# Decoder layer on one core: new prices in the planner that interleaves its side work (table loads, row sums, powers on POOL, the turn back to main matmuls)

## The chip, the cores and the metric

The kernel runs on one core of a Trainium2 chip. The metric is device time in microseconds (us) of one execution. TensorE (PE) multiplies matrices, VectorE (DVE), ScalarE (ACT) and GpSimd (POOL) do the elementwise work, SyncE (SP) issues the transfers.

## What is computed

One decoder layer on 256 rows of width 1024, float32, in three blocks:

```python
h = rms_norm(x, norm_mix_pre)
qa, ka, va, qd, kd, vd, zd, bd, ad, ga, gd = split(h @ w_in)
ya = moba_attention(rope(qa), rope(ka), va)              # 8 heads of 128, causal
yd = gated_deltanet(qd, kd, vd, zd, bd, ad)              # 8 heads of 128, chunks of 64
merged = sigmoid(ga) * (ya @ w_o_attn) + sigmoid(gd) * (yd @ w_o_delta)
x = x + rms_norm(merged @ w_out, norm_mix_post)
h = rms_norm(x, norm_ffn_pre)
out = x + rms_norm((silu(h @ w_gate) * (h @ w_up)) @ w_down, norm_ffn_post)
```

In the gated delta branch q, k and v go through a causal convolution, a silu and, for q and k, a norm over each head; a decay matrix `exp` of cumulative sums gates a chunked recurrence with state S; its output `o` is normalised per head and multiplied by `silu(z)`.

## The kernel before

**Main work.** The large products keep PE busy. Each weight piece of 128x1024 (some of 824 columns) is loaded into one of 4 raw buffers (`wr`), and `split_to` (L427) splits it into a high and a low part, `wh` on ACT and `wl` on DVE, in one of 5 buffers each. A split is asked for three pieces ahead of use. A product takes three matmuls, high x high, high x low and low x high, each of them 256, 412 or 512 columns wide. The main generators (`unit_c`, `unit_z`, `unit_a`, `unit_g`, `unit_oa`, `unit_od`) run over the column blocks of `w_in` and then the output products, and hand control back after every three matmuls.

**Side work.** Between them side generators put small steps: `decays` (L636, decay matrices `d_dc` and their transposes `d_dT`), `dn_tile` (L676, per head group of four and half t of the rows: squares of q and k summed by ACT into `tiny`, the power -1/2 on POOL, the normalised keys `d_kn` on DVE, their transposes, evicted by ACT as `d_kh`, the product of `d_kh` with itself, and a blockwise inverse in `h_a`, `h_T`, `h_U`), `dn_out` (L784, the recurrence: `d_vb`, `h_r`, `d_vn`, state `d_S`, output `d_oA`, whose squares, power and scaling come before its transposes), and `attn` (L892). `q_aq` and `q_ak` are the attention's queries and keys; `q_gt` the sigmoid gates; `scr` takes the squares that nobody reads.

**Order.** A planner, `Flow` (L138), sets the order while the program is written. It keeps a clock for PE (`t`) and one each for ACT, DVE, POOL and the DMA (`clk`). `account` (L165) adds a price to an engine's clock for every operation and notes when its output is ready; `pe` (L196) adds a price to `t` for every matmul. A side generator that has yielded `At(tiles)` gets a due time, the ready time of these tiles plus 50 ns (`MARGIN`, L215). After every three main matmuls `pump` (L228) resumes each side generator whose due time `t` has passed. `issue` (L270) keeps side matmuls behind the last main matmul. The planner's clocks do not wait for buffers of the weights; the framework then lays out each engine's queue, and every engine runs its queue in order. The prices before:

```python
        if kind == "A":
            c = (51 if psum else 94) + 0.833 * n
            c += 93 * sum(isinstance(kw.get(k), bass.AP) for k in ("scale", "bias", "accum_out"))
...
        else:
            c = 90 + (180 * n if ALU.pow in args else 1.15 * n if op == "affine_select" else 1.9 * n)
```

All operations of ACT, DVE, POOL and SP pass through `Engine.__call__` and appear in the profile as L132; matmuls are L290 and transposes L294.

Of the kernel before, what the change touches and what calls it, by code (L numbers as in the profile page):

```python
# [13 lines left out]
AF = mybir.ActivationFunctionType  # L14
ALU = mybir.AluOpType
# [11 lines left out]
NFR = DFF // 512  # L27
PSUM = bass.MemoryType.PSUM
MARGIN = 50
STAG = 0  # L30
WARM = 5
DEC = 6
# [49 lines left out]
class Slots:  # L82
    def __init__(self, pool, name, n, fl):
        self.pool, self.name, self.fl = pool, name, fl
        self.idle = list(range(n))
        self.rel = [0.0] * n
        self.owner = {}
        self.low = n
# [28 lines left out]
def free_size(ap):  # L117
    n = 1
    for d in ap.shape[1:]:
        n *= d  # L120
    return n
# [16 lines left out]
class Flow:  # L138
    def __init__(self):
        self.t = 0.0  # L140
        self.side = []
        self.n = 0
        self.done = set()
        self.log = []
        self.in_side = self.fresh = False
        self.last = None
        self.rdy, self.used = {}, {}
        self.clk = {"A": 0.0, "V": 0.0, "P": 0.0, "D": 1700.0}

# [15 lines left out]
    def account(self, kind, op, args, kw):  # L165
        aps = [a for a in list(args) + list(kw.values()) if isinstance(a, bass.AP)]
        out = kw.get("out", args[0])
        outs = [out]
        if kw.get("accum_out") is not None:
            outs.append(kw["accum_out"])  # L170
        ins = [a for a in aps if all(a is not o for o in outs)]
        n = free_size(out)
        if op == "dma_start":
            st = max(self.clk["D"], self.start(outs, []))
            self.clk["D"] = st + n * 128 * 4 / 341.0
            self.touch(outs, [], self.clk["D"] + 1000, 0)
            return
        psum = any(a.space == PSUM for a in ins)
        if kind == "A":
            c = (51 if psum else 94) + 0.833 * n  # L180
            c += 93 * sum(isinstance(kw.get(k), bass.AP) for k in ("scale", "bias", "accum_out"))
        elif kind == "V":
            if op in ("tensor_copy", "memset", "tensor_scalar"):
                c = 65 + (1.042 if psum else 0.55) * n
            elif op == "scalar_tensor_tensor":
                c = 130 + 1.042 * n
            else:
                n = max([n] + [free_size(a) for a in ins])
                c = 69 + 1.042 * n
        else:  # L190
            c = 90 + (180 * n if ALU.pow in args else 1.15 * n if op == "affine_select" else 1.9 * n)
        st = max(self.clk[kind], self.start(outs, ins))
        self.clk[kind] = st + c
        self.touch(outs, ins, st + c, 60)

    def pe(self, out, l, r, cost):  # L196
        self.t = max(self.t, self.start([out], [l, r])) + cost
        self.touch([out], [l, r], self.t, 200)

# [4 lines left out]
    def step(self, s):  # L204
# [10 lines left out]
        if isinstance(w, At):  # L215
            del s[4:]
            s[0] = max(self.rdy.get(n, 0.0) for n in w.names) + MARGIN
        elif callable(w):
# [34 lines left out]
def build(nc, tc, ctx, A):  # L253
# [756 lines left out]
    def unit_c(u):  # L1010
# [13 lines left out]
        if dns[g] == 6:  # L1024
            fl.add(("dn", g, 0), dn_tile(g, 0))
            fl.add(("dn", g, 1), later(STAG, dn_tile(g, 1)))
            fl.add(("dno", g), after(("dn", g, 0), dn_out, g))
# [327 lines left out]
    def later(ns, gen):  # L1355
        yield ns
        yield from gen

    def after(name, f, *args):
        while name not in fl.done:  # L1360
            yield 500
        yield from f(*args)
# [27 lines left out]
```

## Time and profile before

| | |
|---|---|
| time, median of 3 runs (lowest, highest) | 549.74 us (549.35, 549.91) |
| the profiled execution: time, span | 549.29 us, 547.6 us |
| PE busy, share of the span | 534.8 us, 98% |
| DVE, ACT, POOL busy | 368.1, 315.0, 26.4 us |
| mean granted clock of TensorE, share of full speed | 0.994 |
| ACT table loads | 12, 1283 ns each |
| power on POOL, 128x4 / 128x1, mean | 1012 / 665 ns |

The span runs from the first to the last instruction; the execution's own time is 1.7 us longer. PE is nearly always busy, so an interval in which PE waits is the time that an order can save or lose; the busy time of other engines counts only where PE waits for them.

### The profile page before, as it was taken

The page shows a single profiled execution, that of the slowest core. Times are in us where ns is not written, and L with a number is a line of the kernel's source. Part 1 is how long each engine was busy: PE and PEld are TensorE (multiplying, and loading weights), DVE is VectorE, ACT ScalarE, POOL GpSimd, SP SyncE. Part 2 cuts the span into 40 slices and gives each one's busy share as a digit, 9 for nine tenths or more (in the row PEclk, how much of TensorE's full clock was granted, in tenths as well). Part 3 has the DMA queues.
Part 4 walks back from the last instruction along what each step waited for, and adds up shares of the span by engine and source line. Part 5 has one row for each costly group of instructions (what it writes and reads, how often), then busy time and mean ns, then how long its engine had stood idle before and what let it go on. Part 6 is the DMA issues. An engine that isn't in the chain of part 4 may idle for free.

```text
span 547.6 us, 8378 instructions
## 1 busy us (share of the span) xinstructions
PE 534.8 (98%) x3156; PEld 460.6 (84%) x3156; DVE 368.1 (67%) x650; ACT 315.0 (58%) x553; POOL 26.4 (5%) x38
## 2 busy tenths in 40 slices
PE   7999999899999999999999999999999999999995
PEld 5988898898989888899889988778888888888884
DVE  4899876895879787866577567586465554554434
ACT  6868658487654965786526544585444544443331
POOL 0000002200000230000000000010000000000000
PEclk8999999999999999999999999999999999999998
DMA  8947765245455252244465766257666665555612
GB/s 258 255 149 216 218 197 150 78 117 167 129 168 158 78 167 64 63 148 155 131 201 187 247 210 195 77 158 259 202 189 193 180 197 176 181 189 192 193 38 78
DMA packets 63035, 90.40 MB, mean 165 GB/s; under 512 B 3233, under 2 KB 35090, under 8 KB 62994
## 3 DMA queue, kind: packets, MB, share of 16 engines
q1 hardware_dynamic: 62994, 89.86, 53.4%
q8 instruction: 25, 0.41, 0.3%
q14 instruction: 16, 0.13, 0.1%
HBM read 88.80 MB, written 1.05 MB: 164 GB/s over the span
## 4 chain that ended last, share of the span: by engine, by line
PE 85%; DVE 4%; ACT 3%; DMA 3%; issue 2%; POOL 2%; SPq 0%; POOLq 0%; DVEq 0%; ACTq 0%
PE b_m L290 73%; PE b_s L290 8%; PE b_s L294 2%; PE b_m L294 2%; DMA q_x<-in_x 1%; DVE wl L132 1%; POOL tiny L132 1%; DMA K<-in_shape_k 1%; DMA wr<-in_w_in 1%; ACT wh L132 1%; ACT L132 0%; DVE h_a L132 0%; DVE q_vT L132 0%; SPq L132 0%; ACT d_js L132 0%
## 5 line engine op out<-in xcount | busy, mean ns | idle before, releaser
L132 DVE TENSOR_TENSOR wl<-wr,wh 128x1024 fp32r<-128x1024 f32 (+3 forms) x168 | 197.8, 1184 | 120.8 <-ACT wh L132 116.9
L132 ACT ACTIVATE wh<-wr 128x1024 fp32r<-128x1024 f32 (+3 forms) x168 | 171.8, 1030 | 151.6 <-PE b_m L290 142.9
L290 PE MATMUL b_m<-wh,q_fh 128*128 128x512 f32 x264 | 103.5, 392 | 0.5 <-DVE q_fl L132 0.5
L290 PE MATMUL b_m<-wl,q_fh 128*128 128x512 f32 x264 | 103.0, 390 | 0.0
L290 PE MATMUL b_m<-wh,q_fl 128*128 128x512 f32 x264 | 102.7, 390 | 0.0
L290 PE MATMUL b_m<-wh,q_hh 128*128 128x512 f32 (+2 forms) x208 | 83.1, 400 | 1.0 <-ACT wh L132 1.0
L290 PE MATMUL b_m<-wl,q_hh 128*128 128x512 f32 (+2 forms) x208 | 78.8, 379 | 0.0
L290 PE MATMUL b_m<-wh,q_hl 128*128 128x512 f32 (+2 forms) x208 | 78.8, 379 | 0.0
L290 PEld LDWEIGHTS b_m<-wh,q_fh 128*128 128x128 f32 x264 | 49.6, 188 | 11.0 <-DVE q_fl L132 1.0
L290 PEld LDWEIGHTS b_m<-wl,q_fh 128*128 128x128 f32 x264 | 49.6, 188 | 10.7 <-DVE wl L132 0.7
L290 PEld LDWEIGHTS b_m<-wh,q_fl 128*128 128x128 f32 x264 | 49.5, 188 | 10.3
L290 PE MATMUL b_m<-q_hh,wh 128*128 128x256 f32 x192 | 56.3, 293 | 0.0
L290 PE MATMUL b_m<-q_hl,wh 128*128 128x256 f32 x192 | 54.4, 283 | 0.0
L290 PE MATMUL b_m<-q_hh,wl 128*128 128x256 f32 x192 | 54.4, 283 | 0.0
L290 PEld LDWEIGHTS b_m<-wh,q_hh 128*128 128x128 f32 x208 | 39.5, 190 | 5.4 <-ACT wh L132 1.5
L290 PEld LDWEIGHTS b_m<-wh,q_hl 128*128 128x128 f32 x208 | 39.5, 190 | 5.3
L290 PEld LDWEIGHTS b_m<-wl,q_hh 128*128 128x128 f32 x208 | 39.6, 190 | 4.3 <-DVE wl L132 0.5
L132 POOL TENSOR_TENSOR tiny<-tiny,mhalf 128x4 f32<-128x4 f32 (+1 forms) x20 | 17.4, 873 | 471.3 <-DVE tiny L132 471.3
L290 PEld LDWEIGHTS b_m<-q_hh,wh 128*128 128x128 f32 x192 | 36.7, 191 | 0.4
L290 PEld LDWEIGHTS b_m<-q_hl,wh 128*128 128x128 f32 x192 | 36.7, 191 | 0.3
L290 PEld LDWEIGHTS b_m<-q_hh,wl 128*128 128x128 f32 x192 | 36.7, 191 | 0.1
L132 ACT ACTIVATE h_U<-b_s 128x256 f16<-128x256 f32 (+1 forms) x28 | 11.5, 415 | 10.9 <-PE b_s L290 10.9
(204 smaller groups left out, 718.0 us busy)
## 6 DMA issues: line engine op xcount, KB each, us to landing
wr<-in_w_in SPq DMA_DIRECT2D x56, 512.0 KB, 3.8
wr<-in_w_down SPq DMA_DIRECT2D x22, 512.0 KB, 3.3
wr<-in_w_gate SPq DMA_DIRECT2D x20, 512.0 KB, 3.7
wr<-in_w_up SPq DMA_DIRECT2D x20, 512.0 KB, 3.7
wr<-in_w_in SPq DMA_DIRECT2D x12, 412.0 KB, 3.4
wr<-in_w_o_attn SPq DMA_DIRECT2D x8, 512.0 KB, 4.4
wr<-in_w_o_delta SPq DMA_DIRECT2D x8, 512.0 KB, 4.2
wr<-in_w_out SPq DMA_DIRECT2D x8, 512.0 KB, 3.7
```

Source lines behind the costliest of these rows:

```text
L132: r = f(*args, **kw)
L290: issue(lambda: PE.matmul(out, l, r, start=start, stop=stop))
L294: issue(lambda: PE.transpose(out, in_, idn))
```

## The change

Four prices of the planner change; no instruction is added or taken away. ACT: a sum over a row (`accum_out`) is priced at 205 ns in place of 93, and a pointer as scale or bias at 93, of which the larger one counts; a function of another family than the one before it (`TABLES`: Exp and Sigmoid are one, Silu another) adds 1283 ns. POOL: a power costs 540 + 107 n in place of 90 + 180 n ns, n elements per row. PE: the first main matmul after side matmuls costs 85 ns more.

```diff
--- before.py
+++ after.py
@@ -27,6 +27,7 @@
 NFR = DFF // 512
 PSUM = bass.MemoryType.PSUM
 MARGIN = 50
+TABLES = {AF.Exp: "e", AF.Sigmoid: "e", AF.Silu: "s"}
 STAG = 0
 WARM = 5
 DEC = 6
@@ -142,8 +143,8 @@
         self.n = 0
         self.done = set()
         self.log = []
-        self.in_side = self.fresh = False
-        self.last = None
+        self.in_side = self.fresh = self.turned = False
+        self.last = self.fam = None
         self.rdy, self.used = {}, {}
         self.clk = {"A": 0.0, "V": 0.0, "P": 0.0, "D": 1700.0}
 
@@ -178,7 +179,12 @@
         psum = any(a.space == PSUM for a in ins)
         if kind == "A":
             c = (51 if psum else 94) + 0.833 * n
-            c += 93 * sum(isinstance(kw.get(k), bass.AP) for k in ("scale", "bias", "accum_out"))
+            c += max(93 * any(isinstance(kw.get(k), bass.AP) for k in ("scale", "bias")),
+                     205 * (kw.get("accum_out") is not None))
+            fam = TABLES.get(args[2])
+            if fam and fam != self.fam:
+                self.fam = fam
+                c += 1283
         elif kind == "V":
             if op in ("tensor_copy", "memset", "tensor_scalar"):
                 c = 65 + (1.042 if psum else 0.55) * n
@@ -188,12 +194,15 @@
                 n = max([n] + [free_size(a) for a in ins])
                 c = 69 + 1.042 * n
         else:
-            c = 90 + (180 * n if ALU.pow in args else 1.15 * n if op == "affine_select" else 1.9 * n)
+            c = 540 + 107 * n if ALU.pow in args else 90 + (1.15 * n if op == "affine_select" else 1.9 * n)
         st = max(self.clk[kind], self.start(outs, ins))
         self.clk[kind] = st + c
         self.touch(outs, ins, st + c, 60)
 
     def pe(self, out, l, r, cost):
+        if self.turned and not self.in_side:
+            cost += 85
+        self.turned = self.in_side
         self.t = max(self.t, self.start([out], [l, r])) + cost
         self.touch([out], [l, r], self.t, 200)
```

PE's queue is the same up to about 95 us of the profiled execution and from about 300 us on. Between them, three places.

**PE, the keys of the first head group, around 96 us.** `b4_m` is the main product, `b0_s` and the like are banks of side steps, `d0_kn` and `d1_kn` the normalised keys of the two halves. Before:

```order
L290 MATMUL b4_m_1147<-q4_hh1_126,wl28_1032 128x256
L290 MATMUL b4_m_1147<-q4_hh1_126,wh28_1031 128x256
L290 MATMUL b4_m_1147<-q5_hl1_127,wh28_1031 128x256
L290 MATMUL b4_m_1147<-q4_hh1_126,wl28_1032 128x256
L294 MATMUL b2_s_1180<-ident_71,d0_kn_1130 128x128 x4
L294 MATMUL b3_s_1187<-ident_71,d1_kn_1132 128x128 x4
L294 MATMUL b7_s_1194<-ident_71,q11_aq0_610 128x128 x4
L290 MATMUL b4_m_1147<-q4_hh1_126,wh28_1031 128x256
```

After:

```order
L299 MATMUL b4_m_1147<-q4_hh1_126,wl28_1032 128x256
L303 MATMUL b2_s_1180<-ident_71,q11_aq0_610 128x128 x4
L299 MATMUL b4_m_1147<-q4_hh1_126,wh28_1031 128x256
L299 MATMUL b4_m_1147<-q5_hl1_127,wh28_1031 128x256
L299 MATMUL b4_m_1147<-q4_hh1_126,wl28_1032 128x256
L299 MATMUL b4_m_1147<-q4_hh1_126,wh28_1031 128x256
L299 MATMUL b4_m_1147<-q5_hl1_127,wh28_1031 128x256
L299 MATMUL b4_m_1147<-q4_hh1_126,wl28_1032 128x256
L303 MATMUL b3_s_1192<-ident_71,d0_kn_1136 128x128 x4
L303 MATMUL b7_s_1199<-ident_71,d1_kn_1138 128x128 x4
L303 MATMUL b1_s_1206<-ident_71,q13_ak0_854 128x128 x4
```

The second four `q11_aq0` transposes and six main matmuls now stand ahead of the two groups of key transposes.

**ACT and DVE, the keys of the second head group, around 194 us.** `wh55` to `wh58` are weight pieces, `scr` the squares (bank `b7_s_2263` after, `b0_s_2263` before, for the second half's keys), `h5_r16` reads `d16_vb`. ACT before:

```order
L132 ACTIVATE scr_97,tiny_96<-b0_s_2263 128x128 x3
L132 ACTIVATE d8_dT10_2363<-b2_s_2358 128x512
L132 ACTIVATE h5_r16_2410<-d16_vb_1101 128x512
L132 ACTIVATE q17_ak1_2376<-b3_m_2169,tiny_96 128x512
L132 ACTIVATE wh56_2412<-wr56_2226 128x1024
L132 ACTIVATE wh57_2500<-wr57_2298 128x1024
L132 ACTIVATE d2_vn_2409<-b1_s_2421 128x512
L132 ACTIVATE h6_r16_3098<-d15_vb_2282 128x512
L132 ACTIVATE d4_dc11_2437<-b3_s_2434 128x512
L132 ACTIVATE d3_kh_2445<-b6_s_2440 128x512
L132 ACTIVATE d10_kh_2452<-b4_s_2447 128x512
L132 ACTIVATE wh58_2561<-wr58_2331 128x1024
```

ACT after:

```order
L133 ACTIVATE scr_97,tiny_96<-b7_s_2263 128x128
L133 ACTIVATE q17_ak1_2345<-b5_m_2169,tiny_96 128x512
L133 ACTIVATE scr_97,tiny_96<-b7_s_2263 128x128
L133 ACTIVATE wh56_2409<-wr56_2226 128x1024
L133 ACTIVATE scr_97,tiny_96<-b7_s_2263 128x128
L133 ACTIVATE h6_r16_3101<-d15_vb_2282 128x512
L133 ACTIVATE d14_dT10_2400<-b3_s_2395 128x512
L133 ACTIVATE h5_r16_2451<-d16_vb_1101 128x512
L133 ACTIVATE wh57_2441<-wr57_2298 128x1024
L133 ACTIVATE wh58_2532<-wr58_2331 128x1024
L133 ACTIVATE d2_kh_2432<-b5_s_2427 128x512
L133 ACTIVATE d4_kh_2439<-b3_s_2434 128x512
```

The evictions of the keys (`d2_kh`, `d4_kh`) come after `h5_r16` and two weight pieces, where they (`d3_kh`, `d10_kh`) came ahead of `wh58`. The last square comes after `wh56`.

DVE before:

```order
L132 TENSOR_SCALAR tiny_96<-tiny_96 128x4
L132 SCALAR_TENSOR_TENSOR d16_vb_1101<-b6_s_2342,tiny_96,d16_vb_1101 128x128 x3
L132 TENSOR_SCALAR tiny_96<-tiny_96 128x4
L132 SCALAR_TENSOR_TENSOR d16_vb_1101<-b6_s_2342,tiny_96,d16_vb_1101 128x128
L132 TENSOR_TENSOR d1_oA_2356<-b4_s_2351,tiny_96 128x512
L132 TENSOR_TENSOR d5_kn_2369<-b7_s_2252,tiny_96 128x512
L132 TENSOR_TENSOR d6_kn_2371<-b0_s_2263,tiny_96 128x512
```

DVE after:

```order
L133 SCALAR_TENSOR_TENSOR d16_vb_1101<-b4_s_2376,tiny_96,d16_vb_1101 128x128
L133 TENSOR_TENSOR q17_ak1_2345<-h6_m_2353 128x4x32
L133 TENSOR_SCALAR tiny_96<-tiny_96 128x4
L133 SCALAR_TENSOR_TENSOR d16_vb_1101<-b4_s_2376,tiny_96,d16_vb_1101 128x128
L133 TENSOR_TENSOR d8_kn_2371<-b7_s_2263,tiny_96 128x512
L133 SCALAR_TENSOR_TENSOR d16_vb_1101<-b4_s_2376,tiny_96,d16_vb_1101 128x128 x2
```

The last two of the four quarters of `d16_vb` come after the second `kn`, where all four came ahead of both.

**ACT and DVE, the last output of the second head group, around 295 us.** `d6_oA` before and `d8_oA` after are that output; the squares read it, and DVE's SCALAR_TENSOR_TENSOR on `tiny` reads their sums. ACT before:

```order
L132 ACTIVATE scr_97,tiny_96<-d6_oA_3348 128x128 x4
L132 ACTIVATE wh83_3556<-wr83_3456 128x824
L132 ACTIVATE q12_gt82080_3197<-b2_m_3450,tiny_96 128x412
L132 ACTIVATE q17_gt82081_3199<-b5_m_3451,tiny_96 128x412
L132 ACTIVATE wh84_3581<-wr84_3480 128x1024
L132 ACTIVATE q19_ydh1_3317<-b0_s_3568,colp_95 128x4x128
```

ACT after:

```order
L133 ACTIVATE q12_gt82080_3181<-b0_m_3434,tiny_96 128x412
L133 ACTIVATE q17_gt82081_3183<-b7_m_3435,tiny_96 128x412
L133 ACTIVATE scr_97,tiny_96<-d8_oA_3384 128x128
L133 ACTIVATE wh84_3574<-wr84_3465 128x1024
L133 ACTIVATE scr_97,tiny_96<-d8_oA_3384 128x128 x2
L133 ACTIVATE wh85_3592<-wr85_3483 128x1024
L133 ACTIVATE scr_97,tiny_96<-d8_oA_3384 128x128
L133 ACTIVATE wh86_3617<-wr86_3510 128x1024
L133 ACTIVATE q19_ydh1_3357<-b2_s_3607,colp_95 128x4x128
```

DVE before:

```order
L132 TENSOR_TENSOR d6_oA_3348<-b6_s_3491,d6_oA_3348 128x512
L132 TENSOR_TENSOR wl82_3535<-wr82_3425,wh82_3534 128x824
L132 SCALAR_TENSOR_TENSOR tiny_96<-tiny_96 128x4
L132 TENSOR_SCALAR tiny_96<-tiny_96 128x4
L132 TENSOR_TENSOR tiny_96<-tiny_96 128x4
L132 SCALAR_TENSOR_TENSOR d6_oA_3348<-d6_oA_3348,tiny_96,d7_sz11_2906 128x128 x4
```

DVE after:

```order
L133 TENSOR_TENSOR wl83_3557<-wr83_3440,wh83_3556 128x824
L133 TENSOR_TENSOR d8_oA_3384<-b6_s_3527,d8_oA_3384 128x512
L133 TENSOR_TENSOR wl84_3575<-wr84_3465,wh84_3574 128x1024
L133 TENSOR_TENSOR wl85_3593<-wr85_3483,wh85_3592 128x1024
L133 SCALAR_TENSOR_TENSOR tiny_96<-tiny_96 128x4
L133 TENSOR_SCALAR tiny_96<-tiny_96 128x4
L133 TENSOR_TENSOR tiny_96<-tiny_96 128x4
L133 SCALAR_TENSOR_TENSOR d8_oA_3384<-d8_oA_3384,tiny_96,d7_sz11_2882 128x128 x4
```

The two `q_gt` evictions now precede the squares, two weight pieces lie between the squares, and the DVE operation that reads the sums stands after `wl85`.

## Rows read from the trace of the kernel before

**Rows 1.** The profile's page, part 4: the chain that ended last, by engine.

```profile
PE 85%; DVE 4%; ACT 3%; DMA 3%; issue 2%; POOL 2%; SPq 0%; POOLq 0%; DVEq 0%; ACTq 0%
```

**Rows 2.** Windows: the stretch, its length, busy us of each engine, PE's granted clock.

```profile
core 0: us, PE busy (x) PEld busy (x) DVE busy (x) ACT busy (x) POOL busy (x), PEclk, DMA share, GB/s
95.00:200.00 105.00, 103.25 (x802) 92.74 (x800) 86.61 (x178) 73.99 (x157) 10.08 (x12) 1.00 0.44 130
```

**Rows 3.** Timeline of PE, 96 to 100 us: start, length, instruction, idle before.

```profile
96.60 0.60 PE L294 MATMUL b_s<-ident,d_kn 128*128 128x128 f32 x4
98.52 0.63 PE L294 MATMUL b_s<-ident,d_kn 128*128 128x128 f32 x4 [1.31 <-DVE d_kn L132]
98.98 0.60 PE L294 MATMUL b_s<-ident,q_aq 128*128 128x128 f32 x4
99.34 0.36 PE L290 MATMUL b_m<-q_hh,wh 128*128 128x256 f32 x1
99.54 0.28 PE L290 MATMUL b_m<-q_hl,wh 128*128 128x256 f32 x1
99.66 0.28 PE L290 MATMUL b_m<-q_hh,wl 128*128 128x256 f32 x1
```

**Rows 4.** Timeline of PE, 106 to 107.1 us.

```profile
106.00 0.40 PE L290 MATMUL b_s<-id,h_T 128*128 128x128 f16 x4
106.66 0.40 PE L290 MATMUL b_s<-id,h_T 128*128 128x128 f16 x4 [0.26 <-DVE h_T L132]
106.87 0.36 PE L290 MATMUL b_m<-q_hh,wh 128*128 128x256 f32 x1
107.07 0.28 PE L290 MATMUL b_m<-q_hl,wh 128*128 128x256 f32 x1
```

**Rows 5.** Timeline of PE, 142.5 to 143 us.

```profile
142.68 0.28 PE L290 MATMUL b_m<-q_hh,wl 128*128 128x256 f32 x1
142.99 0.28 PE L290 MATMUL b_s<-h_U,h_a 128*128 128x64 f16 x4
```

**Rows 6.** Timeline of PE, 199 to 203 us.

```profile
199.46 0.40 PE L290 MATMUL b_m<-wh,q_hl 128*128 128x512 f32 x1
200.19 0.66 PE L294 MATMUL b_s<-ident,d_dc 128*128 128x128 f32 x4 [0.34 <-POOL d_dc L132]
200.68 1.95 PE L290 MATMUL b_s<-d_kh 128*128 128x128 f32 x16
```

**Rows 7.** Timeline of DVE, 96 to 98.5 us.

```profile
96.40 0.16 DVE L132 TENSOR_SCALAR tiny<-tiny 128x4 f32<-128x4 f32 x1
97.68 0.69 DVE L132 TENSOR_TENSOR d_kn<-b_s,tiny 128x512 f32<-128x512 f32 x1 [1.12 <-POOL tiny L132]
```

**Rows 8.** Timeline of ACT, 178 to 193 us.

```profile
178.76 0.58 ACT L132 ACTIVATE d_oA<-b_s 128x512 f32<-128x512 f32 x1
...
186.29 1.28 ACT L132 ACT_TABLE_LOAD   x1
187.59 0.60 ACT L132 ACTIVATE d_dc<-b_s 128x512 f32<-128x512 f32 x1
...
192.32 0.19 ACT L132 ACTIVATION_READ_ACCUMULATOR scr<-b_s 128x1 f32 x1
```

**Rows 9.** Groups by line and form: count, busy us, mean ns of one, idle before.

```profile
L132 ACT ACTIVATE wh<-wr 128x1024 fp32r<-128x1024 f32 x146 | 153.9, 1061 | 137.8 <-PE b_m L290 130.6 <-DMA wr<-in_w_in 3.1 <-issue 2.2
L132 ACT ACTIVATE scr<-d_oA 128x128 f32<-128x128 f32 x16 | 4.9, 309 | 0.4
L132 ACT ACTIVATE d_kh<-b_s 128x512 f32<-128x512 f32 x4 | 2.3, 603 | 1.0 <-PE b_s L294 1.0
L132 DVE TENSOR_TENSOR wl<-wr,wh 128x1024 fp32r<-128x1024 f32 x146 | 177.5, 1222 | 113.8 <-ACT wh L132 110.1 <-PE b_m L290 3.5
```

**Rows 10.** Timelines of PE, ACT and DVE, 291 to 299.4 us.

```profile
291.85 1.05 PE L290 MATMUL b_s<-d_vn,d_at 128*128 128x128 f32 x8
...
298.95 0.60 PE L294 MATMUL b_s<-ident,d_oA 128*128 128x128 f32 x4
297.45 1.18 ACT L132 ACTIVATE q_gt<-b_m,tiny 128x412 f32<-128x412 f32 x2 [0.68 <-PE b_m L290]
296.02 0.16 DVE L132 SCALAR_TENSOR_TENSOR tiny<-tiny 128x4 f32<-128x4 f32 x1 [0.58 <-ACT scr L132]
```

## The prediction

> **What bounds the kernel now.** Read the chain of waits first: TensorE (PE) carries 85% of it and no other engine more than 4% [rows 1]. Then the engines by stretch: between 95 and 200 us, where the change moves most, PE is busy 103.25 of 105 us at a granted clock of 1.00, which is the 2.4 GHz level, while DVE has 86.61, ACT 73.99 and POOL 10.08 [rows 2]. So only what adds to or takes from PE's stalls counts. The rest of the working reads PE's timeline place by place, and behind each stall the ACT and DVE rows that end it.
>
> **What the change is, in instructions.** It prices the work; it adds and removes none. ACT's twelve table loads stay twelve. What differs is the order in which each engine meets its work, and so how much main work stands between a side step's producer and its consumer on PE. By the listings nothing moves before about 95 us or after the last normalised output of the second head group (about 300 us). The weight loads keep their queue and their order, and each is issued two to four pieces ahead of its use, so I cost their moves at nothing. At every place below I compare when PE comes (the work ahead of it, at the pace of the rows) with when the operand is there.
>
> **Stalls that go.**
> 1. The second kn tile. The first kn transposes start at 96.60; four at 0.11 us end at 97.04. The second four start at 98.52, so PE loses 1.48 us, and the row names DVE's d_kn [rows 3]. In the new order four q_aq transposes (0.44) and six main matmuls of 0.12 (0.72) precede both. PE then comes 1.16 later, still before the tile, and 0.32 is left. Gain 1.16. Were ACT's rows before it also shifted, the gain lies between 0.8 and 1.48.
> 2. The h_T product: from 106.00 four matmuls of 0.056 end at 106.22; the next group starts at 106.66, after a wait for DVE [rows 4]. The new order puts a whole attention product and six main matmuls between the two. Gain 0.42; that product, over 0.8 us long, is the cover.
> 3. From 142.68 to 142.99 a step takes 0.31 [rows 5] where 0.12 is the pace [rows 3]; one more main group now stands there. Gain 0.19.
> 4. The d_dc transposes of the second half come at 200.19, where the last main matmul, from 199.46 at its pace of 0.23, would have let them start at 199.7: 0.5 lost to POOL [rows 6]. In the new order their chain has more main work in front, but another select runs ahead of theirs on POOL. I take a gain of 0.4, between 0 and 0.5.
>
> Together 2.17 us.
>
> **A stall that comes at the d_kh product (about 198 us).** ACT's queue now reads: the last square of kn's sums, ..., h_r, two weight pieces wh, and only then the two d_kh evictions, which formerly stood ahead of a weight piece. h_r waits for the last quarter of d_vb on DVE, and that stands behind d_kn, which waits for the POOL power. So the two weight pieces and d_kh are queued behind a wait that did not exist, and PE's next side product waits for d_kh.
> When: before, ACT ran from the d_oA eviction at 178.76 to the last square's read-out at 192.32 + 0.19 without a gap, 13.75 us [rows 8]. PE now arrives 1.77 earlier (1 to 3), so the stretch starts at about 177.0; it now also holds two weight pieces and one q_ak eviction that followed it, near 2.6 (a wh is 1.06 alone [rows 9], about 0.1 less behind another). As one piece formerly delayed its start, I take 0.2 off: the last square ends at 193.1. From DVE's small operation to d_kn is 1.28 (96.40 to 97.68), d_kn 0.69 [rows 7], the two d_vb quarters 0.6 (estimate from d_kn, half its width, plus a start each), d_kh 0.60 [rows 9] and h_r, of the same size, as much, two wh 2.0. Sum 5.77, less some 0.1 of overlap at two links: d_kh is there at 198.75. PE is due: 200.68 in the old order [rows 6], less 0.5 of stall 4, less 1.77, less 0.35 (that much less work is listed ahead of it) is 198.06. **Stall 0.7**, range 0 to 2.0, since both ends move if ACT has a gap or a later start.
>
> **A stall that comes at the last d_oA transposes (about 301 us).** Before, the product starts at 291.85 and lasts 8 x 0.11; the transposes start at 298.95, 6.22 later, with no idle time; the q_gt evictions came after ACT's four squares [rows 10]. Now the listing has 36 main matmuls at 0.188 there, 6.79 us. But the squares no longer stand together: ACT does both q_gt evictions, a square, a weight piece, two squares, a weight piece, the last square; and DVE's small operation stands behind the wl of that second piece. Count from the product's end: the second q_gt waits for its bank's last main matmul, three later, and a landing (0.77); q_gt 0.59 (1.18 for two); a square 0.31 with its read-out 0.19, less overlap 0.43; wh 0.96; two squares 0.85; wh 1.06; wl 1.22 [rows 9]; and from the small operation at 296.02 to the transposes at 298.95 another 2.93. Sum 8.8, some 8.7 with the overlap. **Stall 1.9**, range 0.5 to 2.4; below nothing would need the squares to be contiguous again, which the order excludes.
>
> **Price of turning.** After four f32 transposes (from 98.98) the first main matmul comes after 0.36, 0.08 less than four of them take, and the next step is 0.20 instead of 0.12 [rows 3]: net nothing. After 16-bit groups the 0.20 is paid in full [rows 4]. The listing has 48 such groups against 44: 4 x 0.08 = 0.3 lost. Borderline covers elsewhere (I found none short by over 0.1) I put at 0.1.
>
> **A rule against the trace.** The table load at 186.29 takes 1.28 and ACT's next operation starts at 187.59 [rows 8]: a switch costs ACT 1.30 us, nearly what the planner now charges. The Trainium skill (ScalarE: Activation LUTs, "What ACT_TABLE_LOAD costs") adds a drain of about 1.38 us to each load; no row here shows it. By that rule the new price would still be half of the cost and the d_kh stall 1.4 longer, so the sum would be 2.2 instead of 0.8; the rows decide, and I give it no chance.
>
> **Sum.** -2.17 + 0.7 + 1.9 + 0.3 + 0.1 = +0.8 us. The profiled execution took 549.29, so 550.1 on its scale; the median of the runs is 549.74, 0.45 above it, so the forecast is 550.5.
>
> **Rivals.**
> - *The covers hold (faster).* Neither new stall comes: ACT is idle long enough that h_r and the squares find their inputs early. The sum is -2.17 + 0.4 = -1.8, 547.9. For it: all four old stalls are in rows, the new ones are only worked out. Against it: both new ones rest on the order within ACT's queue, which is fixed. If only the d_oA stall fails to come, -1.1: 548.6, at the edge. It decides at the second wh before the last square: should the small DVE operation start within 3.9 us of the product's end, PE does not wait. Chance 0.17 for all of these that end over 0.2% below.
> - *The wait moves up (slower).* The d_kn that waits for POOL also holds d_vb, h_r, two weight pieces and both d_kh. With ACT 1.3 later than I take it, the stall is 2.0, the sum 2.1: 551.8; with the d_oA stall at 2.4 it is 552.4. Everything above 1.1 us counts, which an ACT later by only 0.3 gives. Chance 0.38.
> - *It corrects nothing (no change).* The table of functions calls Sigmoid and Exp one family, though the program loads a table between them, and 0.085 us is charged at f32 returns where rows 3 show none. New stalls then merely replace old ones of like size. My forecast with 0.8 lies here too. Chance 0.45 together.
>
> **How the numbers follow.** A measurement of this kernel can tell about 0.2%, 1.1 us, from no change: 548.64 to 550.84. The forecast lies inside, hence 0.45 same, 0.38 slower, 0.17 faster. The range leaves about one in ten out on each side: below it takes in most of the case without the d_oA stall (548.3), above the longer d_kh wait (552.2).
>
> **What would show it.** In the profile after: the wait of the kn transposes for DVE at 0.3 or less in place of 1.3, no wait for h_T, a wait of TensorE for ACT's d_kh near 198 us and one for DVE's d_oA near 301. Wrong would be: no wait for d_oA there (the order of the squares did not matter), a wait for d_kh beyond 2 us, or a stall at a place named nowhere above.

## The result and the profile after

The changed kernel takes 553.55 us (median of 4 runs, 553.1 to 554.13). The kernel before, run beside it, takes 549.83 (549.35 to 550.01). The ratio is 1.0065, 95% interval 1.0053 to 1.0077: **slower by 3.7 us**. The forecast was 550.5 with a range to 552.2; the time lies above the range. The profiled execution of after took 554.13 and has a span of 551.9, so 4.3 more than the span before. Executions of one kernel differ here by up to 3.3 us, and the profiled ones stand up to 2.1 us apart at 86 us already, where PE's queue is still the same; so a place is judged by the distance between nearby rows of one execution and not by its absolute time. Of the 4.3 us, 0.59 is there before the orders differ: the same main matmul starts at 94.02 before and at 94.61 after. Another, behind the last place of the change, starts at 307.32 and 312.05, so 4.14 is lost in between; 0.36 comes back later.

The chain that ended last, by engine, in the page of after:

```profile
PE 83%; ACT 4%; DVE 4%; issue 3%; POOL 3%; DMA 2%; SPq 0%; DVEq 0%; POOLq 0%; ACTq 0%
```

PE's share was 85% [rows 1]. What PE waits for is in the list of waits of after (us in total, times, longest):

```profile
PE b_s L299 <- ACT d_kh L133: 2.1, 1, 2.1
...
PE b_s L303 <- DVE d_kn L133: 0.8, 2, 0.7
PE b_s L303 <- DVE d_oA L133: 0.7, 1, 0.7
```

The waits left out between them are of the start of the kernel, and before has them too. The wait for d_kh, that for d_oA and 0.66 of the one for d_kn are new. The stretch of [rows 2], and two windows of 2 us behind it (columns as there):

```profile
95.00:200.00 105.00, 103.61 (x804) 93.39 (x802) 84.72 (x175) 71.44 (x156) 11.48 (x12) 1.00 0.44 128
200.00:202.00 2.00, 0.43 (x2) 0.43 (x3) 2.00 (x4) 2.00 (x4) 0.00 (x0) 0.86 0.37 27
202.00:204.00 2.00, 2.00 (x10) 1.90 (x10) 1.40 (x3) 0.00 (x1) 0.00 (x0) 0.50 0.96 337
```

Up to 200 us PE does well: PE is busy 0.36 us more than in the same stretch before, at the same clock. Then it stands nearly still for 2 us, and in the 2 us after that it looks fully busy but runs at a granted clock of 0.50, the 1.2 GHz level. PE's timeline at the places of the argument:

```profile
98.35 0.60 PE L303 MATMUL b_s<-ident,d_kn 128*128 128x128 f32 x4
99.10 0.63 PE L303 MATMUL b_s<-ident,d_kn 128*128 128x128 f32 x4 [0.16 <-DVE d_kn L133]
...
196.85 0.60 PE L303 MATMUL b_s<-ident,d_kn 128*128 128x128 f32 x4
198.11 0.63 PE L303 MATMUL b_s<-ident,d_kn 128*128 128x128 f32 x4 [0.66 <-DVE d_kn L133]
...
199.03 0.40 PE L299 MATMUL b_m<-wh,q_hl 128*128 128x512 f32 x1
201.57 2.08 PE L299 MATMUL b_s<-d_kh 128*128 128x128 f32 x8 [2.14 <-ACT d_kh L133]
203.30 0.77 PE L299 MATMUL b_m<-wh,q_hh 128*128 128x512 f32 x1
...
207.16 0.66 PE L303 MATMUL b_s<-ident,d_dc 128*128 128x128 f32 x4
...
307.30 0.35 PE L299 MATMUL b_m<-wh,q_hl 128*128 128x412 f32 x1
308.35 1.02 PE L303 MATMUL b_s<-ident,d_oA 128*128 128x128 f32 x4 [0.69 <-DVE d_oA L133]
309.13 0.44 PE L299 MATMUL b_m<-wh,q_hh 128*128 128x412 f32 x1
```

Read against the pace: the first pair of kn transposes is 0.75 apart where four take 0.44, so 0.31 is lost; it was 1.48 [rows 3]. A like pair in the second head group loses 1.26 - 0.44 = 0.82, which before it did not. The d_kh product should start 0.23 after 199.03 and starts 2.31 later than that; its eight matmuls then take 1.73 to the next row. The last d_oA transposes should start at 307.49; they start at 308.35, and since their fourth tile waits too, 0.78 passes to the next main matmul where 0.36 is usual: 1.28 lost. The waits of PE for h_T [rows 4] and for d_dc at this place [rows 6] are gone: after the matmul at 206.90 the d_dc transposes follow at 207.16, 0.26 later, where the pace is 0.23.

**Why d_kh comes late.** Behind it are the queues of DVE, POOL and ACT. DVE first:

```profile
185.30 1.22 DVE L133 TENSOR_TENSOR wl<-wr,wh 128x1024 fp32r<-128x1024 f32 x1
186.44 0.69 DVE L133 TENSOR_TENSOR d_gm<-K,ghi 128x512 fp32r<-128x512 f32 x1
187.04 0.69 DVE L133 TENSOR_TENSOR d_gm<-K,glo 128x512 fp32r<-128x512 f32 x1
188.63 0.24 DVE L133 TENSOR_SCALAR tiny<-tiny 128x4 f32<-128x4 f32 x2 [0.90 <-POOL tiny L133]
...
189.99 0.59 DVE L133 TENSOR_SCALAR tiny<-tiny 128x4 f32<-128x4 f32 x1 [0.99 <-POOL tiny L133]
...
192.64 0.69 DVE L133 TENSOR_TENSOR d_kn<-b_s,tiny 128x512 f32<-128x512 f32 x1 [1.12 <-POOL tiny L133]
...
195.99 0.16 DVE L133 TENSOR_SCALAR tiny<-tiny 128x4 f32<-128x4 f32 x1
...
197.27 0.69 DVE L133 TENSOR_TENSOR d_kn<-b_s,tiny 128x512 f32<-128x512 f32 x1 [0.87 <-POOL tiny L133]
```

POOL in the same stretch:

```profile
185.47 3.12 POOL L133 TENSOR_TENSOR tiny<-tiny,mhalf 128x4 f32<-128x4 f32 x1 [2.73 <-DVE tiny L133]
188.94 1.01 POOL L133 TENSOR_TENSOR tiny<-tiny,mhalf 128x4 f32<-128x4 f32 x1 [0.35 <-DVE tiny L133]
```

And ACT:

```profile
192.45 0.27 ACT L133 ACTIVATION_READ_ACCUMULATOR scr<-b_s 128x1 f32 x1
...
198.51 0.63 ACT L133 ACTIVATE h_r<-d_vb 128x512 bf16<-128x512 f32 x1 [1.23 <-DVE d_vb L133]
199.04 1.99 ACT L133 ACTIVATE wh<-wr 128x1024 fp32r<-128x1024 f32 x2
200.94 1.06 ACT L133 ACTIVATE d_kh<-b_s 128x512 f32<-128x512 f32 x2
```

ACT ends the last square of the keys at 192.45 + 0.27 = 192.72; the prediction had 193.1. But DVE takes up the small operation that needs it only at 195.99, 3.27 us later. DVE's queue is in order, and three waits for POOL stand ahead in it. Two, at 188.63 and 189.99, are for powers of the *queries'* norms, the first of which takes 3.12 us instead of 1.01. The third, at 192.64, is for the power of the first half's keys. What DVE then has to catch up (a `wl` piece, the rotation of `q_ak`) stands ahead too. From there all goes as forecast (power, d_kn at 197.27, d_vb, h_r, two weight pieces, d_kh): 5.58 us from the small operation to the d_kh product.

The two waits for the queries' powers are not new. DVE's timeline before:

```profile
187.14 0.17 DVE L132 TENSOR_SCALAR tiny<-tiny 128x4 f32<-128x4 f32 x1 [1.05 <-POOL tiny L132]
188.12 0.17 DVE L132 TENSOR_SCALAR tiny<-tiny 128x4 f32<-128x4 f32 x1 [0.81 <-POOL tiny L132]
...
192.61 0.15 DVE L132 TENSOR_SCALAR tiny<-tiny 128x4 f32<-128x4 f32 x1
```

They cost 1.86 there and 1.89 after, yet before the small operation follows the end of the last square (192.51) by 0.1. New ahead of it are the third wait (1.12) and two `d_gm`, which before ran at 178.64 and 180.38, ahead of the queries' powers. After, DVE stood idle there for 2.57 us, until 180.15, waiting for a `wh` of ACT.

### The profile page after: what moved, and what is told of

The parts are those of the page before. It is cut to its first block, busy times and chain, and to the rows that moved or that the text cites. A ratio compares the mean times of both kernels' runs of the same rounds, so it can differ in the third digit from the quotient of the medians.

```text
span 551.9 us, 8375 instructions
## 1 busy us (share of the span) xinstructions
PE 538.0 (97%) x3156; PEld 462.1 (84%) x3156; DVE 368.6 (67%) x650; ACT 313.6 (57%) x553; POOL 28.1 (5%) x38
## 4 chain that ended last, share of the span: by engine, by line
PE 83%; ACT 4%; DVE 4%; issue 3%; POOL 3%; DMA 2%; SPq 0%; DVEq 0%; POOLq 0%; ACTq 0%
PE b_m L299 71%; PE b_s L299 9%; POOL tiny L133 2%; PE b_m L303 2%; PE b_s L303 2%; ACT wh L133 1%; DMA q_x<-in_x 1%; DVE wl L133 1%; DMA wr<-in_w_in 1%; DVE tiny L133 1%; DVE d_vb L133 1%; ACT scr L133 1%; ACT L133 0%; DVE q_vT L133 0%; SPq L133 0%
## 5 line engine op out<-in xcount | busy, mean ns | idle before, releaser
L133 POOL TENSOR_TENSOR tiny<-tiny,mhalf 128x4 f32<-128x4 f32 (+1 forms) x20 | 19.6, 978 | 472.9 <-DVE tiny L133 472.9
L133 ACT ACT_TABLE_LOAD x12 | 15.4, 1283 | 3.8 <-PE b_m L299 1.9
```

Of the source, the lines that this page charges most:

```text
L133: r = f(*args, **kw)
```

## The experiments

The theory has three mechanisms, and each can be taken out alone: ACT's queue order (d_kh behind h_r and two weight pieces), DVE's queue order (the keys' small operation behind the queries' powers), and the order of the squares at the end. The rivals are that contention on POOL, or the clock alone, carries the loss. In the edits, `issue_after(x)` puts the instructions in its block behind x in their engine's queue.

**1. d_kh ahead of h_r and of the weight pieces on ACT.** `behind_kh()` is `issue_after` of the last d_kh eviction.

```diff
-            ACT.activation(hi, r, AF.Copy)
+            with behind_kh() if j in (57, 58) else ExitStack():
+                ACT.activation(hi, r, AF.Copy)
...
-        ACT.activation(kh, v4(b), AF.Copy)
+        kh_ev[g, t] = ACT.activation(kh, v4(b), AF.Copy).ins
...
-            ACT.activation(r16, vb, AF.Copy)
+            with behind_kh() if (g, t) == (0, 1) else ExitStack():
+                ACT.activation(r16, vb, AF.Copy)
```

> The changed kernel with one edit: on ACT the two d_kh evictions of the second head group come ahead of h_r and of the weight pieces 57 and 58, as they came ahead of piece 58 in the kernel before. Theory A (ACT's order is what TensorE waits for at 198 to 202 us): the wait for d_kh falls from 2.1 us to under 0.3, the granted clock stays at 1.00 from 200 to 206 us, and the time falls by 3 to 4 us, to about 550. The wait for d_kn just before (0.7 us) stays. Theory B (DVE's lag behind the POOL powers is what counts, whatever ACT's order): h_r then comes late instead, its consumer waits, and the time falls by less than 2 us. Theory C (the slow matmuls from 201.6 to 205 us have nothing to do with the wait): the clock still falls to 0.5 there.

Measured: 550.48 us (549.87 to 551.1, 10 runs), beside a kernel before of 550.19; ratio 1.0004 (0.9994 to 1.0013). That is 3.1 less than after. The edit moves three instructions of ACT's queue; a few that come later (two d_kh matmuls of PE, a `d_vb` and a `wl` of DVE, a select of POOL) change places with them. PE's timeline:

```profile
197.79 0.60 PE L303 MATMUL b_s<-ident,d_kn 128*128 128x128 f32 x4
199.05 0.63 PE L303 MATMUL b_s<-ident,d_kn 128*128 128x128 f32 x4 [0.67 <-ACT d_kh L133]
...
199.98 0.40 PE L299 MATMUL b_m<-wh,q_hl 128*128 128x512 f32 x1
200.22 1.06 PE L299 MATMUL b_s<-d_kh 128*128 128x128 f32 x8
```

The window behind it:

```profile
202.00:204.00 2.00, 2.00 (x17) 1.82 (x15) 2.00 (x6) 1.70 (x3) 0.17 (x1) 1.00 0.80 204
```

The kn pair still loses 0.82 (the row names ACT's first d_kh, which there ends within 0.1 of the late d_kn), the d_kh product follows without a stop, and the clock stays at 1.00. The last d_oA wait (0.69) is still there. So the wait for d_kh, with the clock where it falls behind it, is most of the loss.

**2. The queries' powers behind the keys' kn on DVE**, in the second head group.

```diff
-        DVE.tensor_tensor(kn, v4(bk), rk[:, :, None].to_broadcast([128, 4, 128]), op=ALU.mult)
+        kn_ev[g, t] = DVE.tensor_tensor(kn, v4(bk), rk[:, :, None].to_broadcast([128, 4, 128]), op=ALU.mult).ins
...
-            DVE.tensor_scalar(rq2, ssq[:, c0:c0 + 4], EPS, None, op0=ALU.add)
+            with tc.issue_after(kn_ev[g, 1]) if g in (1,) and (g, 1) in kn_ev else ExitStack():
+                DVE.tensor_scalar(rq2, ssq[:, c0:c0 + 4], EPS, None, op0=ALU.add)
```

> The changed kernel with one edit: DVE's small operation that starts the power for the q norms of the second head group, which nobody needs before 226 us, comes behind the last d_kn instead of ahead of the k norms. ACT's order is untouched: h_r and two weight pieces still precede d_kh. Theory A (ACT's order): the wait for d_kh stays above 1.2 us, the clock still falls, the time falls by at most 1.5 us. Theory B (DVE stood 3.3 us behind its last square because two powers on POOL, one of them 3.1 us long, were ahead of it): the small operation of the last d_kn moves from 196.0 to 193.5 or earlier, the wait for d_kn (0.7) goes, the wait for d_kh falls under 0.4, the clock stays at 1.00, and the time falls by 3.5 to 4.5 us, to about 549.5.

Measured: 553.39 (552.44 to 554.71, 4 runs), ratio 1.0061 (1.0038 to 1.0084), no better than after. The small operation comes 1.00 after the end of the last square instead of 3.27 (at 194.22, where 193.5 or earlier was expected); the kn wait is gone and d_kh's shrinks to 0.73. But the two powers now run beside the weights' `wl` and take 2.96, DVE waits for them, and its `h_a` ends only at 204.73. POOL's queue is in order, and its select of d_dc stands behind the one of `h_a`; PE waits for it (two rows of POOL's timeline, then one of PE's):

```profile
198.60 2.96 POOL L133 TENSOR_TENSOR tiny<-tiny,mhalf 128x4 f32<-128x4 f32 x2 [3.13 <-DVE tiny L133]
204.81 0.64 POOL L133 TENSOR_SCALAR_AFFINE_SELECT h_a<-h_a 128x512 f16<-128x512 f16 x1 [3.25 <-DVE h_a L133]
```

```profile
206.09 0.74 PE L303 MATMUL b_s<-ident,d_dc 128*128 128x128 f32 x4 [2.08 <-POOL d_dc L133]
```

The wait moved to another consumer, and the clock fell behind it (0.51 between 208 and 210 us).

**3. The same powers behind the tile `at`**, later still. The edit is that of experiment 2 with another instruction to stand behind:

```diff
-        DVE.tensor_tensor(at, v4(b), decayT[g, t], op=ALU.mult)
+        at_ev[g, t] = DVE.tensor_tensor(at, v4(b), decayT[g, t], op=ALU.mult).ins
...
+            with tc.issue_after(at_ev[g, 1]) if g in (1,) and (g, 1) in at_ev else ExitStack():
```

> The changed kernel with the powers of the q norms of the second head group put behind the last step of its key tile on DVE (the product with d_dT), so that they stand in front of nothing at all between 184 and 210 us. The run with these powers just behind the last d_kn took 2.1 us from the select of d_dc on POOL instead. Theory B (DVE's lag behind POOL): no wait for d_kn, the wait for d_kh 0.7 to 1.0 us as in that run, no wait for d_dc over 0.5, the clock at 1.00 in most executions, and a time 2 to 3.5 us below the changed kernel, 550.0 to 551.5. Theory A (ACT's order alone): a wait for d_kh over 1.5 us, and no more than 1 us is won.

Measured: 550.45 (549.39 to 551.29, 10 runs) beside 549.8, ratio 1.0014 (1.0005 to 1.0023): 3.1 less than after. DVE's timeline, then PE's:

```profile
194.56 0.16 DVE L133 TENSOR_SCALAR tiny<-tiny 128x4 f32<-128x4 f32 x1
```

```profile
197.68 1.03 PE L303 MATMUL b_s<-ident,d_kn 128*128 128x128 f32 x8
...
200.15 1.16 PE L299 MATMUL b_s<-d_kh 128*128 128x128 f32 x8 [0.73 <-ACT d_kh L133]
```

Without the queries' powers ahead of it, the small operation starts 1.01 after the end of the last square (193.55) instead of 3.27, all eight kn transposes run as one, and **the wait for d_kh is 0.7** (0.90 lost against the pace, where after loses 2.31). So DVE's queue behind POOL makes most of that stall, and either edit, 1 or 3, takes most of the loss away, since it takes both queues to make it. What ACT's order costs with DVE in time was not tried: 1.0 of the lag is left here, with DVE's wait for the first half's power (1.13) still ahead. That the 0.7 equals the forecast is therefore in part luck.

**4. The queries' powers apart from DVE's two-input work**, still ahead of the keys' part.

```diff
-            DVE.tensor_scalar(rq2, ssq[:, c0:c0 + 4], EPS, None, op0=ALU.add)
+            with tc.issue_after(gm_ev[1, 1]) if g == 1 else ExitStack():
+                DVE.tensor_scalar(rq2, ssq[:, c0:c0 + 4], EPS, None, op0=ALU.add)
```

> The changed kernel with DVE's start of both q powers put behind the two d_gm products, so that no DVE operation with two tensors from SBUF runs beside the first power. If those operations held POOL up, the two powers take 1.0 us each instead of 3.1 and 1.0. The queue behind them waits anyway: DVE reaches q_ydl at 190.7 as before, and TensorE's waits for d_kn (0.7) and d_kh (2.1) stay within 0.3 us. If the 3.1 us has another cause, it stays.

Measured: 553.31 in a single run, too few for a verdict (after: 553.1 to 554.13). POOL:

```profile
187.27 1.99 POOL L133 TENSOR_TENSOR tiny<-tiny,mhalf 128x4 f32<-128x4 f32 x2 [5.06 <-DVE tiny L133]
```

The long power is gone: two take 1.99 together. But the small operation still comes 3.11 after the end of the last square (192.19 to 195.30), where after has 3.27. PE waits 2.15 for d_kh and 0.53 for kn (after: 2.14 and 0.66), and the clock falls here too. So the contention on POOL does not carry the loss; that the powers stand ahead in DVE's queue does.

**5. Work in the place of the wait.** 34 16-bit matmuls on constant masks ahead of this one d_kh product; they add work that the result does not use, as they write a bank that the product then overwrites.

```diff
+        for i in range(34 if (g, t) == (1, 0) else 0):
+            issue(lambda: PE.matmul(b[:, 0:128], id16, mask16, start=True, stop=True))
```

> The changed kernel with 34 short matmuls (16 bit, 128 columns, some 0.056 us each, 1.9 us together) into the bank of the d_kh product, ahead of it, so that TensorE has work while it waits for d_kh. Their result is overwritten. Theory (the wait lets TensorE's clock fall, and the fall costs 1.5 to 1.8 us beyond the wait): granted clock 1.00 from 200 to 206 us, the d_kh product starts when it did (201.6), and the time falls by 1.4 to 1.8 us, to about 552. Rival (the matmuls behind the wait are slow for another reason, the transfers that run at the same time): the clock or the pace stays as it was and the time is unchanged or longer by up to 0.3 us.

Measured: 553.31 (552.6 to 554.34, 4 runs), ratio 1.0059 (1.0039 to 1.0078).

```profile
200.82 2.07 PE L723 MATMUL b_s<-mask,id 128*128 128x128 f16 x34
203.11 1.16 PE L299 MATMUL b_s<-d_kh 128*128 128x128 f32 x8 [0.22 <-ACT d_kh L133]
```

The product starts 2.53 after the last main matmul (200.58), as in after (2.54). The clock stays 1.00 from 200 to 208 us, and the product takes 1.16. One execution does not show that the work is what kept the clock up: experiment 6 has 1.00 without it. Nor does the median show the expected gain: 0.24 less than after is within the spread.

**6. The four squares of the last d_oA together**, two weight pieces put behind them.

```diff
-            ACT.activation(hi, r, AF.Copy)
+            with tc.issue_after(sq_ev[1, 1]) if j in (84, 85) else ExitStack():
+                ACT.activation(hi, r, AF.Copy)
...
-                ACT.activation(scr, oA[:, h, :], AF.Square, accum_out=sso[:, h:h + 1])
+                sq_ev[g, t] = ACT.activation(scr, oA[:, h, :], AF.Square, accum_out=sso[:, h:h + 1]).ins
```

> The changed kernel with one edit: on ACT the weight pieces 84 and 85 come behind the four squares of the last d_oA, so these stand together again. Theory A (the two pieces between the squares, and the wl ahead of DVE's small operation, make the wait of TensorE at 308 us): the last d_oA transposes start without a wait, the time falls by 1.2 to 1.4 us, to about 552.2. Rival (it is the late q_gt evictions, which still come first): at most 0.4 us is won.

Measured: 553.56 (551.53 to 554.73, 4 runs), ratio 1.0069 (1.0043 to 1.0095); the median is that of after, so the expected gain of 1.2 to 1.4 does not show in it. PE's timeline in its profile, taken in the fastest of the four runs, decides two things:

```profile
201.57 1.16 PE L299 MATMUL b_s<-d_kh 128*128 128x128 f32 x8 [2.14 <-ACT d_kh L133]
...
205.86 0.66 PE L303 MATMUL b_s<-ident,d_dc 128*128 128x128 f32 x4
...
306.18 0.60 PE L303 MATMUL b_s<-ident,d_oA 128*128 128x128 f32 x4
```

First, the d_oA wait is gone while the q_gt evictions still come first, so the squares' order did cause it. Second, up to 207 us this program is the one of after: the same wait, and d_kh at the same 201.57. Here the clock stayed at 1.00 and the d_dc transposes start at 205.86 instead of 207.16. **The drop of the clock cost 1.30 us** in the profiled execution of after; it comes in some executions and not in others. Transfers are not what slows the product: between 202 and 204 us the DMA share is 0.99 here and 0.96 in after. At full clock d_dc loses 0.25 at this place (0.48 after the main matmul at 205.38, where the pace is 0.23).

**7. Experiments 1, 3 and 6 together**, with the queries' powers moved in both head groups: the diffs of 1, 3 and 6, and

```diff
-            with tc.issue_after(at_ev[g, 1]) if g in (1,) and (g, 1) in at_ev else ExitStack():
+            with tc.issue_after(at_ev[g, 1]) if g in (0, 1) and (g, 1) in at_ev else ExitStack():
```

> The changed kernel with three edits together: d_kh ahead of h_r and the weight pieces on ACT, the squares of the last d_oA together, and the q powers of both head groups behind the last step of their key tiles. If the stalls are what was found, the waits for d_kn, d_kh and d_oA between 95 and 310 us are all under 0.3 us and the clock stays at 1.00; what is left of the change is its gain of 1.7 us before 175 us and the first kn wait (0.3), less some 0.6 for more turns and small waits. That is 1.0 to 1.7 us below the kernel before, about 548.9. If a new wait comes (POOL's selects, or weight pieces late on DVE), it is equal to the kernel before.

Measured: 548.45 (547.61 to 549.47, 11 runs) beside 549.8 (548.71 to 550.54, 26 runs); ratio 0.998 (0.9971 to 0.9989). **It is faster than both kernels**, by 1.35 than the one before and by 5.1 than after. Of PE's waits for d_kn, d_kh, d_oA and d_dc only this is left in the list of waits:

```profile
PE b_s L303 <- POOL d_dc L133: 0.2, 1, 0.2
```

PE has 92% of the chain that ended last (85% before).

**8. Only the queries' powers moved, in the kernel before** (the edit of 3, with both groups as in 7, made in the kernel before).

> The kernel before, with its prices, and only the q powers of both head groups put behind the last step of their key tiles. If DVE's queue behind POOL's powers is also what made the old stall at the second kn tile (1.5 us at 98 us), this falls to 0.5 or less and the time by 0.8 to 1.3 us, to about 549.1. If that stall is ACT's squares, nothing changes.

Measured: 549.52 (548.43 to 550.57, 11 runs), ratio 0.9996 (0.9985 to 1.0006): no change. The kn wait of [rows 3] shrinks from 1.3 to 0.2, but PE's timeline shows a wait that was not there:

```profile
111.85 0.28 PE L290 MATMUL b_s<-h_T,wl 128*128 128x64 f16 x4
112.67 0.28 PE L290 MATMUL b_s<-wl,h_T 128*128 128x64 f16 x4 [0.53 <-DVE wl L132]
```

These products start 0.82 apart where the pace is 0.12, so 0.7 of the 1.1 gained is given back some 13 us on.

**9 to 12. One price at a time.** Each kernel keeps one of the four new prices; the other three are as before.

```diff
-            c += max(93 * any(isinstance(kw.get(k), bass.AP) for k in ("scale", "bias")),
-                     205 * (kw.get("accum_out") is not None))
+            c += 93 * sum(isinstance(kw.get(k), bass.AP) for k in ("scale", "bias", "accum_out"))
-            fam = TABLES.get(args[2])
-            if fam and fam != self.fam:
-                self.fam = fam
-                c += 1283
...
-            c = 540 + 107 * n if ALU.pow in args else 90 + (1.15 * n if op == "affine_select" else 1.9 * n)
+            c = 90 + (180 * n if ALU.pow in args else 1.15 * n if op == "affine_select" else 1.9 * n)
...
-        if self.turned and not self.in_side:
-            cost += 85
```

These are the four reversals; each kernel has three of them.

Only the sums over a row:

> The kernel before with only the price of sums over a row changed (205 for a sum, 93 for pointers, the larger). By its listing this price alone brings the three things seen in the changed kernel: the q_aq transposes ahead of the first kn tiles, h_r and weight pieces 57 and 58 ahead of d_kh on ACT, and weight pieces between the last squares; but both q powers stand ahead of d_gm on DVE. If these orders are what costs, waits for d_kh (1 to 2 us) and for the last d_oA (0.5 to 1.3) show again, and the time is 0.5 to 3 us above the kernel before. If the four prices only do harm together, it is within 0.5 us of it.

Only the table loads:

> The kernel before with only the table loads priced. By its listing the first kn tiles keep their old order, so the old wait of 1.3 us at 98 us stays; d_kh stands behind h_r but ahead of weight piece 57; the squares of the last d_oA are split once. A wait for d_kh of 0 to 1 us, no large wait at the last d_oA, time within 1.2 us of the kernel before.

Only the power:

> The kernel before with only the price of the power on POOL changed. Its queues differ from the kernel before in few places; the old wait at the second kn tile stays. Time within 0.6 us of the kernel before. If POOL's lag is what the planner had to know, this price alone should win 1 us or more.

Only the turn:

> The kernel before with only the 85 ns for the turn from side to main matmuls. PE's clock in the planner then runs ahead of TensorE, so side steps come after fewer main matmuls: the kn tiles now stand ahead of the q_aq transposes. The wait at the second kn tile grows from 1.3 to between 1.8 and 2.8 us, the waits near 200 us grow too, and the time is 1 to 4 us above the kernel before. If the turn is paid in full on the chip, waits shrink and the time falls.

Measured, 4 runs each, beside a kernel before of 549.8:

| new price kept | us (lowest, highest) | ratio (95%) | PE's largest new or remaining waits, us |
|---|---|---|---|
| sums over a row | 553.77 (552.34, 554.58) | 1.0071 (1.0048, 1.0094) | d_kh 2.1, d_oA 1.1 |
| table loads | 554.15 (553.38, 554.58) | 1.0084 (1.0062, 1.0105) | d_kn 3.1 in two, d_dc 1.0 |
| power on POOL | 553.77 (553.04, 554.25) | 1.0073 (1.0053, 1.0093) | d_dc 1.8, d_kn 1.3 |
| turn to main | 556.66 (556.01, 559.24) | 1.0136 (1.0106, 1.0165) | d_kn 3.0 in two, d_oA 1.2 |

A row of PE's timeline for each of the last three, in the table's order:

```profile
198.44 0.66 PE L300 MATMUL b_s<-ident,d_kn 128*128 128x128 f32 x4 [1.81 <-DVE d_kn L133]
```

```profile
204.56 0.66 PE L296 MATMUL b_s<-ident,d_dc 128*128 128x128 f32 x4 [1.84 <-POOL d_dc L133]
```

```profile
98.91 1.09 PE L298 MATMUL b_s<-ident,d_kn 128*128 128x128 f32 x4 [2.40 <-DVE d_kn L133]
```

All four missed in time. The sums cost 4.0 us where 0.5 to 3 was expected, though their two waits came about as expected; table loads and power cost 4.4 and 4.0 where at most 1.2 and 0.6 was expected, and the turn 6.9 where 1 to 4 was. The four singles add up to 19 us and all four together cost 3.7, so the costs do not add: each new set of prices gives a new order, and each of these four orders has some consumer waiting that did not wait before. The waits of the table do not make up the whole of each cost; the rest was not traced. Why the planner foresees none of these waits was not tried; its clocks wait for no weight buffer and know of no contention between POOL and DVE.

## Why the prediction was wrong

- *Gains.* Right. The second kn tile: 1.48 to 0.31, forecast 0.32 left. h_T: its wait is gone (0.42). d_dc: 0.5 to 0.25 at full clock (experiment 6), a gain of 0.25 where 0.4 was forecast; in the profile of after it is under 0.1, because the slow clock lets PE come later. The third, at 142.68 (0.19), is too small to follow in the new order. Together some 1.8 of 2.17.
- *The stall at d_kh.* **The step that failed is "the last square ends at 193.1" with DVE's small operation right behind it.** The square ended at 192.72; DVE was not free. The prediction followed ACT's queue up to the square and DVE's from the small operation on, and did not read what stands ahead of that operation in DVE's own queue. Three waits for POOL stand there. Measured: the small operation 3.27 after the square, and 2.31 lost instead of 0.7. Experiment 3 takes two of the waits away and loses 0.90. Of the rivals, the one where the wait moves up named this stall (2.0), with a late ACT as the cause, which the rows do not show: the late engine was DVE. Two of the prediction's own signs of being wrong came: a wait for d_kh beyond 2 us, and a stall at a place that it had not named.
- *A place named nowhere.* The same late d_kn stops PE by itself, 0.82 at 198.11. The prediction used this d_kn only as a link to d_kh; its own consumer on PE was put at nothing.
- *The clock.* Not in the prediction: 1.30 more in the profiled execution of after.
- *The last d_oA transposes.* Mechanism right (experiment 6), size off: 1.28 instead of 1.9. The mis-sized term is the 2.93 from the small operation to the transposes, read from [rows 10]. That was the distance to where PE came, not the length of the chain. After, with PE waiting, it is 308.35 - 306.17 = 2.18. The terms ahead of it come 0.4 shorter than forecast, and the wait of the fourth tile, which the prediction does not have, adds 0.4:

```profile
306.17 0.16 DVE L133 SCALAR_TENSOR_TENSOR tiny<-tiny 128x4 f32<-128x4 f32 x1
```

- *Turning and small covers.* 0.4 was forecast. Of the 4.14 lost between 94 and 312 us, 0.2 is left once the terms are added (-1.8 + 2.3 + 0.8 + 1.3 + 1.3 = 3.9). The 0.59 of the start stands apart from this.
- *The rule on table loads.* After, too, a load lasts 1.28, and the next operation follows 1.29 after its start; the drain of 1.38 that the Trainium skill (ScalarE: Activation LUTs, "What ACT_TABLE_LOAD costs") adds is not seen here either (the load at 185.66, d_dc at 186.95).

So the signs of the named places that can be followed were right. The sum failed because two of the four losses came from one queue, read from its middle, and a third, the clock, hangs on them.

## What to carry to other kernels

When an order changes, follow the late operand back through *every* in-order queue on its way: the question is not when its input is ready but what stands ahead of it on its own engine, and whether that waits for a third engine. A distance between two rows is the length of a chain only if its last link waited; otherwise it is the consumer's own time. More accurate prices do not make a better order by themselves: here each of four, taken alone, brought new waits, while moving a few instructions by hand beat both kernels.

## What the hardware showed

- **POOL beside DVE.** The same 128x4 power took 1.01 us alone and 3.12 while DVE ran a `wl` and two `d_gm`, each with two inputs in SBUF, from 185.30 to 187.7; two together took 1.99 once that work was done and 2.96 beside a `wl` (experiments 4 and 2). DVE's next operation, at 188.63, shows that the long span was real. The Trainium skill (GPSIMD Engine Reference, section 1, Specifications) says that this engine shares its SBUF interfaces with VectorE and contends with DVE instructions that have two SBUF inputs; the rows agree, and add that a small power can take three times as long.
- **The clock behind a wait.** After PE's wait of 2.14 us the granted clock was 0.50 for 202 to 204 us in the execution of after, and 1.00 in that of experiment 6 behind the same wait. It also fell behind waits of 2.08 and 2.15 us (experiments 2 and 4). With small matmuls in the stop (experiment 5) it stayed at 1.00; whether they are the reason is not shown. Where it fell, the stop cost 1.30 us more than its own length.
